# Two heads' scores in one two-bank PSUM tile, their six matmuls tied in order

## The chip, the cores and the metric

The kernel runs on one core of one Trainium2 chip. What counts is device time in microseconds (us) of one execution, the median of several runs. The core's engines run side by side, each through its own queue in order: PE (TensorE: matmuls and transposes into PSUM; PEld is its weight load), DVE (VectorE), ACT (ScalarE), POOL (GpSimd) and SP (which here issues most transfers). PSUM has 8 banks; one bank holds 512 fp32 numbers in each of 128 partitions.

## The reference

Two decoder layers over 512 positions of width 1024, all fp32. Layer 0 (mLSTM heads and pooling groups) is not touched. Layer 1, cut to what matters:

```python
q = rmsnorm(q.reshape(hd), g_q)                  # 16 heads x 64
k = rmsnorm((ckv @ w_uk).reshape(hd), g_k); v = (ckv @ w_uv).reshape(hd)
...
score = einsum('bqh,bqhs->bqs', wib, relu(einsum('bqhd,bsd->bqhs', qib, ki)))   # 4 index heads x 64
_, idx = lax.top_k(score, 128)                   # per query, causal
logits = einsum('bqhd,bqkhd->bqhk', qb, k[idx]) * 64 ** -0.5 + bias[idx]
out = softmax(logits) @ v[idx]
return x + (out * silu(z)) @ w_out
```

## The kernel before

Each fp32 matrix is split into a high and a low part (`_h`, `_l`), and a product takes three matmuls: high by high, high by low, low by high. The kernel computes all causal keys and masks those that the top-k leaves out.

Layer 1 runs by the list `ORDER` of steps: `i` (index scores of one block of 128 queries), `s` (top-k rounds on DVE), `q`, `k`, `v`, `z` (projections), `a` (attention of four heads for one block) and `y` (splitting the gated result for the output projection). Below that list a scheduler orders each engine's instructions: it lays out what is ready by priorities and its own estimate of time, and takes a tile from its pool when a buffer comes free. So an edit at one place can move instructions at others.

`head_pair` (L663) makes the scores of two heads, e = 0 and e = 1. A head has 64 channels, so head 0 lies on partitions 0 to 63 of `q` and `k` and head 1 on 64 to 127, and each matmul uses 64 rows of the array (the shape is shown as 64*128). Two banks of the pool `qk` (`qk=2`, L610) take the heads, one each; the loop writes the matmuls alternately, but the scheduler is free to put others between. `scores` (L676) calls it twice for each of the blocks 1 to 3 and reads each head with a Relu on ACT (L689). `attend` (L784) calls it twice per step, 32 times in all; each head's bank is read by one DVE instruction (L808: it adds the mask and bias tile `cb`, `sel` or `twin` and takes the extreme), then come the exponential (ACT L810), a reciprocal (DVE L811), a scaling (ACT L812), transposes (PE L820, pool `tr`, two banks), their split (ACT L116, DVE L113), the product with v (PE L829 to L831, pool `po`, one bank), and the gate (DVE L835).

With n the number of keys, 256, 384 or 512, there are 38 pairs. The six matmuls of a pair are called here step A (k high, q high), B (k low, q high) and C (k high, q low), each for two heads.

The last projection (`dense_ch4`, L202, called at L852) accumulates four output tiles in two banks of `mm` and two of `qk`; `store` (L845) reads each (L848).

Of the kernel before, what the change touches and what calls it, by code (L numbers as in the profile page):

```python
# [2 lines left out]

# [5 lines left out]
F32 = mybir.dt.float32  # L9
# [49 lines left out]
def trunk(ctx: ExitStack, tc: tile.TileContext, a: dict, out: bass.AP):  # L59
    nc = tc.nc  # L60
    V, A, G, T = nc.vector, nc.scalar, nc.gpsimd, nc.tensor
# [5 lines left out]
    ps = {}  # L67
    ps_pools = ExitStack()

    def psum_pools(**banks):  # L70
        ps_pools.close()
        ps.clear()
        for n, b in banks.items():
            ps[n] = ps_pools.enter_context(tc.tile_pool(name="ps_" + n, bufs=b, space=PSUM))
# [4 lines left out]
    def bank(n):  # L79
        return ps[n].tile([128, 512], F32, name=n)  # L80

    def mm():
        return bank("mm")
# [51 lines left out]
    def wtile(shape, loads, queue=nc.sync):  # L135
        n = math.prod(shape)
        raw = wp.tile([128, 1024], F32, name="raw", bufs=3)
        wh = wp.tile([128, 1024], F32R, name="wh")
        wl = wp.tile([128, 1024], F32R, name="wl")

        def view(t):
            t = t[:, :n]
            if len(shape) == 2:
                t = t.rearrange("p (x y) -> p x y", x=shape[0])
            return t
        for sl, src in loads:
            queue.dma_start(view(raw)[:, sl[0], sl[1]], src)
        A.copy(wh[:, :n], raw[:, :n])  # L148
        low_engine[0].tensor_tensor(wl[:, :n], raw[:, :n], wh[:, :n].bitcast(F32), op=ALU.subtract)  # L149
        return view(wh), view(wl)  # L150
# [3 lines left out]
    def wrows(w, r0, nk, c0, n):  # L154
        return w[r0:r0 + 128 * nk, c0:c0 + n].rearrange("(k p) c -> p k c", p=128)
# [8 lines left out]
    def dense_tok(act, ks, cols, evac, groups=(range(NT),)):  # L164


        n = sum(x[2] for x in cols)
        step = min(1024 // n, len(ks))
        ws = {}
        for tts in groups:  # L170
            acc = {t: mm() for t in tts}
            for k0 in range(0, len(ks), step):
                kk = ks[k0:k0 + step]
                if k0 not in ws:
                    ws[k0] = wcols(cols, kk)
                wh, wl = ws[k0]
                for t in tts:
                    for j, k in enumerate(kk):
                        ah, al = act(k)
                        ts = slice(128 * t, 128 * t + 128)  # L180
                        first, last = (k0 + j == 0), (k0 + j == len(ks) - 1)
                        T.matmul(acc[t][:, :n], ah[:, ts], wh[:, j], start=first, stop=False)  # L182
                        T.matmul(acc[t][:, :n], ah[:, ts], wl[:, j], start=False, stop=False)  # L183
                        T.matmul(acc[t][:, :n], al[:, ts], wh[:, j], start=False, stop=last)  # L184
                    if k0 + step >= len(ks):
                        evac(t, acc[t])
# [7 lines left out]
    def part_ch(act, w, ks, ps):  # L194
        wh, wl = w
        for j, k in enumerate(ks):
            ah, al = act(k)
            T.matmul(ps, wh[:, j], ah, start=(k == 0), stop=False)  # L198
            T.matmul(ps, wh[:, j], al, start=False, stop=False)  # L199
            T.matmul(ps, wl[:, j], ah, start=False, stop=(k == NK - 1))  # L200

    def dense_ch4(act, w, hf, evac, alloc):  # L202

        acc = [alloc(c) for c in range(4)]
        for k0 in range(0, NK, 2):
            wh, wl = wtile([2, 512], [((ALL, ALL), wrows(w, 128 * k0, 2, 512 * hf, 512))])
            for c in range(4):
                cs = slice(128 * c, 128 * c + 128)
                part_ch(act, (wh[:, :, cs], wl[:, :, cs]), (k0, k0 + 1), acc[c])
                if k0 == NK - 2:  # L210
                    evac(4 * hf + c, acc[c])
# [8 lines left out]
    xn = lambda k: (xn_h[:, k], xn_l[:, k])  # L220
# [105 lines left out]
    w_in, w_out = a["e_w_in"], a["e_w_out"]  # L326
# [280 lines left out]

    w_in, w_out = a["o_w_in"], a["o_w_out"]
    w_uk, w_uv = a["o_w_uk"], a["o_w_uv"]
    psum_pools(mm=2, bg=1, qk=2, tr=2, po=1)  # L610
    GR = ((0, 1), (2, 3))
    p2 = ctx.enter_context(tc.tile_pool(name="p2", bufs=1))
    zy = p2.tile([128, 8, S], F32, name="zy")
# [46 lines left out]
    def ckv_proj():  # L660
        dense_tok(xn, range(NK), [(w_in, 1024, 256)], ev_ckv, GR)

    def head_pair(q, k, n):  # L663

        p = [bank("qk"), bank("qk")]
        for j in range(3):
            for e in range(2):
                es = slice(64 * e, 64 * e + 64)
                T.matmul(p[e][:, :n], q(es, j), k(es, j), start=(j == 0), stop=(j == 2))  # L669
        return p  # L670

    near = {0: tmask}
    far = {}
# [2 lines left out]
    def scores(i):  # L676
        n = 128 * (i + 1)
        qs = slice(128 * i, 128 * i + 128)
        acc = sel[i] = (p2 if i == 3 else p1).tile([128, n], F32, name=f"sel{i}")
        G.memset(acc[:, :n - 128], 0.0)  # L680
        G.tensor_copy(acc[:, n - 128:], tmask)
        pair = {}
        for h in range(4):
            if h % 2 == 0:
                pair = head_pair(lambda e, j: (qi_h, qi_h, qi_l)[j][e, h // 2, qs],
                                 lambda e, j: (ki_h, ki_l, ki_h)[j][e, :n], n)
            p = pair[h % 2]
            rl = t1.tile([128, 512], F32, name="relu", tag="cb")
            A.activation(rl[:, :n], p[:, :n], AF.Relu)  # L689
            V.scalar_tensor_tensor(acc, rl[:, :n], wi[:, i, h:h + 1], acc, op0=ALU.mult, op1=ALU.add)  # L690
# [93 lines left out]
    def attend(c, i):  # L784
# [6 lines left out]
        for pr in range(2):  # L791
            probs = []
            pq = head_pair(lambda e, j: (q_h, q_h, q_l)[j][e, pr, qs], lambda e, j: (k_h, k_l, k_h)[j][e, pr, :nn], nn)
            for e in range(2):
                hd = 2 * pr + e
# [46 lines left out]
    step = dict(i=scores, c=ckv_proj, q=q_proj, k=k_proj, v=v_proj, z=z_proj, s=select, a=attend, y=y_split)  # L842
# [6 lines left out]
        nc.scalar.dma_start(out[128 * c:128 * c + 128], o)  # L849

    for hf in range(2):
        dense_ch4(xn, w_out, hf, store, lambda c: bank(("mm", "qk", "mm", "qk")[c]))  # L852


def layout(inputs):
# [34 lines left out]
```

## Time and profile before

| | before |
|---|---|
| median of 3 runs | 774.74 us (774.5 to 776.12) |
| the profiled execution | 773.58 us, of which the span from first to last instruction 771.8 us |
| PE busy | 751.6 us (97%) |
| DVE, ACT, POOL busy | 464.8 (60%), 398.1 (52%), 304.7 us (39%) |
| chain that ended last | PE 84%, DVE 9% |

Layer 1's attention work stands between 488 and 740 us of the span, the last projection mostly behind it. "Busy" of PE counts a matmul from its start to its modelled end, and matmuls overlap; what one costs is read from the distance between the starts of neighbours.

### The profile page before, as it was taken

Reading aid. Unit: us, or ns where it says so; the run is one execution under the profiler, and the core shown is the slowest. Engines: PE = TensorE matmul, PEld = TensorE weight load, DVE = VectorE, ACT = ScalarE, POOL = GpSimd, SP = SyncE. Lnnn points to the kernel's source line nnn. Section 1 sums busy time; section 2 is a strip of 40 time slices with the busy share of each in tenths; the row PEclk is TensorE's granted clock in tenths of the full one; section 3 lists DMA queues with packets and bytes.
Section 4 is the critical chain, followed back from the end, with each engine's and each line's share of the span. In section 5 each row is a group of like instructions: output and inputs, shape, how many; then the busy total and the mean of one; then the engine's idle time right before and its main releaser. Section 6 shows DMA issues by size and latency. Waiting matters only on the chain.

```text
span 771.8 us, 11177 instructions
## 1 busy us (share of the span) xinstructions
PE 751.6 (97%) x4123; PEld 631.6 (82%) x4123; DVE 464.8 (60%) x988; ACT 398.1 (52%) x778; POOL 304.7 (39%) x246
## 2 busy tenths in 40 slices
PE   7989999999999999999999999998999999999988
PEld 5887888887888889888888888987788888887766
DVE  6686534344727765147224572599999978877531
ACT  6445333282445543355433353545667688887620
POOL 5545448732003020131363393445124555472241
PEclk9999999999999999999999999999999999999999
DMA  7523342345332313332322244422321221020051
GB/s 222 155 75 84 84 108 74 105 122 150 106 86 69 87 63 110 82 96 87 89 84 61 88 154 123 111 69 69 82 69 42 69 69 55 9 91 13 28 192 54
DMA packets 83990, 69.20 MB, mean 90 GB/s; under 512 B 3884, under 2 KB 71900, under 8 KB 83936
## 3 DMA queue, kind: packets, MB, share of 16 engines
q1 hardware_dynamic: 82144, 65.83, 29.6%
q10 hardware_dynamic: 1760, 2.66, 1.0%
q8 instruction: 32, 0.52, 0.3%
q14 instruction: 22, 0.18, 0.1%
q0 software_dynamic: 32, 0.01, 0.0%
HBM read 64.25 MB, written 4.23 MB: 89 GB/s over the span
## 4 chain that ended last, share of the span: by engine, by line
PE 84%; DVE 9%; ACT 2%; DMA 2%; issue 2%; POOL 1%; SPq 1%; DVEq 0%; ACTq 0%; POOLq 0%
PE mm L198 13%; PE mm L199 13%; PE mm L200 12%; PE mm L182 8%; PE mm L183 8%; PE mm L184 8%; PE qk L669 5%; PE tr L820 2%; PE po L829 2%; PE po L831 2%; DVE sel L698 1%; DVE m L697 1%; DMA raw<-in_e_w_in_dram 1%; PE po L830 1%; DVE wl L149 1%
## 5 line engine op out<-in xcount | busy, mean ns | idle before, releaser
L149 POOL TENSOR_TENSOR wl<-raw,wh 128x1024 fp32r<-128x1024 f32 (+4 forms) x65 | 148.7, 2290 | 274.4 <-ACT wh L148 230.6
L148 ACT CAST wh<-raw 128x1024 fp32r<-128x1024 f32 (+4 forms) x117 | 113.4, 971 | 172.8 <-PE mm L199 52.3
L198 PE MATMUL mm<-xn_h,wh 128*128 128x512 f32 x336 | 132.8, 397 | 3.1 <-DVE v_l L363 2.0
L200 PE MATMUL mm<-xn_h,wl 128*128 128x512 f32 x336 | 132.6, 395 | 0.0
L199 PE MATMUL mm<-xn_l,wh 128*128 128x512 f32 x336 | 132.3, 394 | 0.0
L183 PE MATMUL mm<-wl,xn_h 128*128 128x256 f32 (+2 forms) x384 | 123.9, 323 | 0.0
L184 PE MATMUL mm<-wh,xn_l 128*128 128x256 f32 (+2 forms) x384 | 123.2, 322 | 0.0
L182 PE MATMUL mm<-wh,xn_h 128*128 128x256 f32 (+2 forms) x384 | 121.6, 325 | 1.0 <-DVE xT L595 0.9
L149 DVE TENSOR_TENSOR wl<-raw,wh 128x1024 fp32r<-128x1024 f32 (+2 forms) x52 | 66.0, 1269 | 63.2 <-ACT wh L148 62.7
L182 PEld LDWEIGHTS mm<-wh,xn_h 128*128 128x128 f32 x384 | 72.0, 189 | 9.2 <-ACT wh L148 1.3
L183 PEld LDWEIGHTS mm<-wl,xn_h 128*128 128x128 f32 x384 | 72.3, 188 | 7.0 <-issue 1.1
L184 PEld LDWEIGHTS mm<-wh,xn_l 128*128 128x128 f32 x384 | 72.2, 188 | 6.7 <-issue 0.7
L198 PEld LDWEIGHTS mm<-xn_h,wh 128*128 128x128 f32 x336 | 63.2, 189 | 17.1 <-DVE v_l L363 2.1
L199 PEld LDWEIGHTS mm<-xn_l,wh 128*128 128x128 f32 x336 | 63.3, 188 | 14.5 <-issue 0.6
L200 PEld LDWEIGHTS mm<-xn_h,wl 128*128 128x128 f32 x336 | 63.3, 188 | 13.8
L200 PE MATMUL mm<-y_h,wl 128*128 128x512 f32 x128 | 50.1, 393 | 0.6 <-DVE wl L149 0.6
L199 PE MATMUL mm<-y_l,wh 128*128 128x512 f32 x128 | 50.4, 394 | 0.0
L198 PE MATMUL mm<-y_h,wh 128*128 128x512 f32 x128 | 48.9, 395 | 0.9 <-ACT y_h L116 0.9
L504 DVE SCALAR_TENSOR_TENSOR cv<-mm,s_conv,cv 128x511 f32<-128x511 f32 (+2 forms) x48 | 35.9, 747 | 16.3 <-ACT cv L502 15.3
L810 ACT ACTIVATE lg<-lg,st 128x128 f32<-128x128 f32 (+3 forms) x64 | 35.8, 561 | 6.1 <-DVE st L808 5.9
L812 ACT ACTIVATE lg<-lg,st 128x128 f32<-128x128 f32 (+3 forms) x64 | 34.0, 557 | 7.4 <-DVE st L811 7.4
L805 POOL TENSOR_TENSOR cb<-sel,abias 128x256 f32<-128x256 f32 x32 | 24.5, 770 | 30.1 <-DVE st L808 22.1
(272 smaller groups left out, 1578.0 us busy)
## 6 DMA issues: line engine op xcount, KB each, us to landing
raw<-in_e_w_in_dram SPq DMA_DIRECT2D x52, 512.0 KB, 3.8
raw<-in_o_w_in_dram SPq DMA_DIRECT2D x18, 512.0 KB, 3.9
raw<-in_e_w_out_dram SPq DMA_DIRECT2D x16, 512.0 KB, 3.8
raw<-in_o_w_out_dram SPq DMA_DIRECT2D x8, 512.0 KB, 3.6
xT<-in_xT_dram SPq DMA_DIRECT2D x8, 256.0 KB, 4.2
x_one<-xT SPq DMA_DIRECT2D x8, 256.0 KB, 3.0
abias<-lines SPq DMA_DIRECT2D x4, 512.0 KB, 4.2
o_sb<-x_one SPq DMA_DIRECT2D x8, 256.0 KB, 4.4
```

The costliest lines, as they stand in the source:

```text
L148: A.copy(wh[:, :n], raw[:, :n])
L149: low_engine[0].tensor_tensor(wl[:, :n], raw[:, :n], wh[:, :n].bitcast(F32), op=ALU.subtract)
L182: T.matmul(acc[t][:, :n], ah[:, ts], wh[:, j], start=first, stop=False)
L183: T.matmul(acc[t][:, :n], ah[:, ts], wl[:, j], start=False, stop=False)
L184: T.matmul(acc[t][:, :n], al[:, ts], wh[:, j], start=False, stop=last)
L198: T.matmul(ps, wh[:, j], ah, start=(k == 0), stop=False)
L199: T.matmul(ps, wh[:, j], al, start=False, stop=False)
L200: T.matmul(ps, wl[:, j], ah, start=False, stop=(k == NK - 1))
L504: V.scalar_tensor_tensor(u[:, j:], ps[:, :S - j], w[:, 3 - j:4 - j], u[:, j:], op0=ALU.mult, op1=ALU.add)
L669: T.matmul(p[e][:, :n], q(es, j), k(es, j), start=(j == 0), stop=(j == 2))
L810: A.activation(lg[:, :n], lg[:, :n], AF.Exp, scale=-1.0, bias=st[:, 0:1], accum_out=st[:, 1:2])
L812: A.activation(lg[:, :n], lg[:, :n], AF.Copy, scale=st[:, 2:3])
```

## The change

The pool `qk` now holds one tile of two banks in place of two tiles of one bank. `head_pair` takes that one tile, head e in bank e. A new function `together` issues the six matmuls in the order A0 A1 B0 B1 C0 C1: each but the first is created under high priority, and each is tied to the one before it by a dependency without a semaphore (`NoSync`), which fixes the order on the engine and adds no wait. The tile comes free when both heads have been read. In the last projection both `qk` accumulators of one half (output tiles 1 and 3 of four) share such a tile.

```diff
-    psum_pools(mm=2, bg=1, qk=2, tr=2, po=1)
+    psum_pools(mm=2, bg=1, qk=1, tr=2, po=1)
...
+    def together(steps):
+
+        last = steps[0]()
+        for step in steps[1:]:
+            with tc.high_priority():
+                ins = step()
+            tc.add_manual_dep(ins.ins, last.ins.name, mybir.DependencyInfo(
+                mybir.DependencyClass.NoSync, mybir.DependencyReason.DATA), reason="together")
+            last = ins
+
     def head_pair(q, k, n):
 
-        p = [bank("qk"), bank("qk")]
-        for j in range(3):
-            for e in range(2):
-                es = slice(64 * e, 64 * e + 64)
-                T.matmul(p[e][:, :n], q(es, j), k(es, j), start=(j == 0), stop=(j == 2))
-        return p
+        p = ps["qk"].tile([128, 2, 512], F32, name="qk")
+        rows = (slice(0, 64), slice(64, 128))
+        together([partial(T.matmul, p[:, e, :n], q(es, j), k(es, j), start=(j == 0), stop=(j == 2))
+                  for j in range(3) for e, es in enumerate(rows)])
+        return p[:, 0], p[:, 1]
...
     for hf in range(2):
-        dense_ch4(xn, w_out, hf, store, lambda c: bank(("mm", "qk", "mm", "qk")[c]))
+        two = ps["qk"].tile([128, 2, 512], F32, name="qk")
+        dense_ch4(xn, w_out, hf, store, lambda c: two[:, c // 2] if c % 2 else mm())
```

No instruction is added or taken away. On every engine the order up to the first index scores is the same; behind them it differs on PE, DVE, ACT and POOL. In the changed file lines up to L608 move down by one, the score matmuls stand at L666 and L669, and lines from L672 on move down by ten (L808 is L818, L835 is L845).

**Place 1, PE, a pair of 256 keys in the second group of four heads.** Before (`mm` is another projection's accumulator, `qk_5697` and `qk_5698` are the two heads' banks):

```order
L183 MATMUL mm_5971<-wl_6005,xn_h_84 128x256
L669 MATMUL qk_5697<-ak_h_4891,aq_h_4973 128x256
L669 MATMUL qk_5697<-ak_l_4892,aq_h_4973 128x256
L669 MATMUL qk_5697<-ak_h_4891,aq_l_4974 128x256
L182 MATMUL mm_5972<-wh_5974,xn_h_84 128x256
L183 MATMUL mm_5972<-wl_5975,xn_h_84 128x256
L669 MATMUL qk_5698<-ak_h_4891,aq_h_4973 128x256
L669 MATMUL qk_5698<-ak_l_4892,aq_h_4973 128x256
L669 MATMUL qk_5698<-ak_h_4891,aq_l_4974 128x256
L184 MATMUL mm_5972<-wh_5974,xn_l_85 128x256
```

The same pair in the changed kernel:

```order
L185 MATMUL mm_5412<-wh_5371,ckv_l_4075 128x256
L666 MATMUL qk_5684<-ak_h_4885,aq_h_4967 128x256
L669 MATMUL qk_5684<-ak_h_4885,aq_h_4967 128x256
L669 MATMUL qk_5684<-ak_l_4886,aq_h_4967 128x256 x2
L669 MATMUL qk_5684<-ak_h_4885,aq_l_4968 128x256 x2
L183 MATMUL mm_5953<-wh_5956,xn_h_84 128x256
```

Two stretches of three with two projection matmuls between became one stretch of six. Of the 38 pairs, 37 now stand as such a stretch, and one of 512 keys is cut into AABB and CC; before, the 228 score matmuls stood in 65 stretches.

**Place 2, PE, a pair of 256 keys in the third group of heads.** Before (two banks, head after head, nothing between):

```order
L184 MATMUL mm_6722<-wh_6754,xn_l_85 128x256
L669 MATMUL qk_6483<-ak_h_5374,aq_h_5969 128x256
L669 MATMUL qk_6483<-ak_l_5375,aq_h_5969 128x256
L669 MATMUL qk_6483<-ak_h_5374,aq_l_5970 128x256
L669 MATMUL qk_6484<-ak_h_5374,aq_h_5969 128x256
L669 MATMUL qk_6484<-ak_l_5375,aq_h_5969 128x256
L669 MATMUL qk_6484<-ak_h_5374,aq_l_5970 128x256
```

The same pair in the changed kernel:

```order
L183 MATMUL mm_6778<-wh_6726,xn_h_84 128x256
L666 MATMUL qk_6460<-ak_h_5366,aq_h_5951 128x256
L669 MATMUL qk_6460<-ak_h_5366,aq_h_5951 128x256
L669 MATMUL qk_6460<-ak_l_5367,aq_h_5951 128x256 x2
L669 MATMUL qk_6460<-ak_h_5366,aq_l_5952 128x256 x2
L841 MATMUL po_6332<-pt_l_6339,av_h_6113 128x256
```

Head after head became step after step. Five pairs stand before as this one does.

**Place 3, PE and DVE, from the last pair of 256 keys (query block 1) of the last group to the next pair.** PE before, from the pair's head 1 to head 0 of the next (`qk_7227`, in the bank that `qk_7185`, head 0, held):

```order
L669 MATMUL qk_7186<-ak_h_6175,aq_h_6719 128x256
L669 MATMUL qk_7186<-ak_l_6176,aq_h_6719 128x256
L669 MATMUL qk_7186<-ak_h_6175,aq_l_6720 128x256
L831 MATMUL po_7005<-pt_l_7025,av_h_6131 128x256
L820 MATMUL tr_7071<-cst_72,lg_7042 128x128
L820 MATMUL tr_7071<-cst_72,lg_7049 128x128
L820 MATMUL tr_7071<-cst_72,lg_7042 128x128
L820 MATMUL tr_7071<-cst_72,lg_7049 128x128
L829 MATMUL po_7055<-pt_h_7061,av_h_6881 128x256
L830 MATMUL po_7055<-pt_h_7061,av_l_6882 128x256
L669 MATMUL qk_7227<-ak_h_6175,aq_h_6719 128x384
```

PE in the changed kernel:

```order
L669 MATMUL qk_7152<-ak_h_6157,aq_l_6692 128x256 x2
L841 MATMUL po_6975<-pt_l_6995,av_h_6113 128x256
L830 MATMUL tr_7040<-cst_72,lg_7011 128x128
L830 MATMUL tr_7040<-cst_72,lg_7018 128x128
L830 MATMUL tr_7040<-cst_72,lg_7011 128x128
L830 MATMUL tr_7040<-cst_72,lg_7018 128x128
L839 MATMUL po_7024<-pt_h_7030,av_h_6853 128x256
L840 MATMUL po_7024<-pt_h_7030,av_l_6854 128x256
L666 MATMUL qk_7193<-ak_h_6157,aq_h_6691 128x384
L669 MATMUL qk_7193<-ak_h_6157,aq_h_6691 128x384
```

DVE before, and then in the changed kernel, around the reads of that pair (`ISA` is L808's instruction and, on a row without `lg`, the reading of its extreme):

```order
L835 TENSOR_TENSOR zy_3890<-po_7005,zy_3890 64x128 x2
L808 ISA lg_7195,st_7196<-qk_7185,cb_7193 128x256
L808 ISA st_7196 128x1
L113 TENSOR_TENSOR pt_l_7062<-tr_7056,pt_h_7061 128x512
L808 ISA lg_7203,st_7204<-qk_7186,cb_7201 128x256
```

```order
L845 TENSOR_TENSOR zy_3890<-po_6975,zy_3890 64x128 x2
L818 ISA lg_7161,st_7162<-qk_7152,cb_7159 128x256
L818 ISA st_7162 128x1
L818 ISA lg_7169,st_7170<-qk_7152,cb_7167 128x256
L818 ISA st_7170 128x1
```

The work between two pairs on PE is the same; before, the next pair's first head needed one read done (of `qk_7185`, whose scores stand eleven rows above the first one shown), now it needs both reads of the pair just computed.

## Rows read from the trace of the kernel before

**Rows 1.** The page: busy time, share of the span and instructions of each engine.
```profile
PE 751.6 (97%) x4123; PEld 631.6 (82%) x4123; DVE 464.8 (60%) x988; ACT 398.1 (52%) x778; POOL 304.7 (39%) x246
```
**Rows 2.** Busy time by stretch: us, per engine with instructions, PE clock, DMA.
```profile
488.00:546.90 58.90, 56.88 (x363) 49.13 (x361) 51.82 (x138) 29.55 (x67) 25.87 (x18) 0.97 0.26 72
546.90:624.50 77.60, 76.32 (x508) 65.96 (x507) 74.33 (x213) 54.46 (x128) 32.49 (x38) 1.00 0.22 60
624.50:740.20 115.70, 112.41 (x734) 92.25 (x732) 84.00 (x271) 92.00 (x223) 56.06 (x62) 1.00 0.16 54
```
**Rows 3.** What PE waited for, 546.9 to 740.2: us, times, longest.
```profile
PE po L829 <- DVE zy L835: 2.2, 4, 1.3
PE mm L182 <- DVE av_l L113: 1.1, 2, 0.8
PE mm L198 <- ACT xn_h L116: 1.1, 1, 1.1
```
**Rows 4.** The score matmuls of step A by size, durations in ns.
```profile
L669 PE MATMUL qk<-ak_h,aq_h x76: 380/437/502, 488.8 to 723.8; 64*128 64x256 f32 x36, 64*128 64x384 f32 x20, 64*128 64x512 f32 x20
```
**Rows 5.** PE in time: start us, us, what; two heads together, 256 keys.
```profile
488.49 0.28 PE L183 MATMUL mm<-wl,xn_h 128*128 128x256 f32 x1
488.61 0.28 PE L184 MATMUL mm<-wh,xn_l 128*128 128x256 f32 x1
488.81 0.39 PE L669 MATMUL qk<-ak_h,aq_h 64*128 64x256 f32 x2
...
489.36 0.38 PE L182 MATMUL mm<-wh,xn_h 128*128 128x256 f32 x1
```
**Rows 6.** PE in time, two heads apart, 256 keys (place 1).
```profile
609.80 0.38 PE L669 MATMUL qk<-ak_h,aq_h 64*128 64x256 f32 x1
...
610.35 0.39 PE L182 MATMUL mm<-wh,xn_h 128*128 128x256 f32 x1
...
610.77 0.38 PE L669 MATMUL qk<-ak_h,aq_h 64*128 64x256 f32 x1
...
611.32 0.38 PE L184 MATMUL mm<-wh,xn_l 128*128 128x256 f32 x1
```
**Rows 7.** PE in time, one head of 384 keys, then one of 512.
```profile
681.31 0.44 PE L669 MATMUL qk<-ak_h,aq_h 64*128 64x384 f32 x1
...
682.03 0.39 PE L182 MATMUL mm<-wh,ckv_h 128*128 128x256 f32 x1
...
649.64 0.50 PE L669 MATMUL qk<-ak_h,aq_h 64*128 64x512 f32 x1
...
650.53 0.39 PE L184 MATMUL mm<-wh,xn_l 128*128 128x256 f32 x1
```
**Rows 8.** PE in time, the untied pair of place 2.
```profile
660.33 0.39 PE L669 MATMUL qk<-ak_h,aq_h 64*128 64x256 f32 x2
...
660.88 0.55 PE L820 MATMUL tr<-cst,lg 128*128 128x128 f32 x3
```
**Rows 9.** PE, then DVE in time, at place 3.
```profile
707.26 0.39 PE L831 MATMUL po<-pt_l,av_h 128*128 128x256 f32 x1
...
708.42 0.36 PE L829 MATMUL po<-pt_h,av_h 128*128 128x256 f32 x1 [0.34 <-DVE zy L835]
...
707.69 0.59 DVE L835 TENSOR_TENSOR zy<-po,zy 64x128 f32<-64x128 f32 x2 [2.18 <-PE po L831]
708.31 0.42 DVE L808 CUSTOM_DVE_ANT_0 lg<-qk,cb 128x256 f32<-128x256 f32 x1
708.66 0.08 DVE L808 DVE_READ_ACCUMULATOR2_ANT st<- 128x1 f32 x1
```
**Rows 10.** DVE in time, a read that came late, of scores begun at 683.16.
```profile
688.37 0.54 DVE L808 CUSTOM_DVE_ANT_0 lg<-qk,cb 128x384 f32<-128x384 f32 x1
```
**Rows 11.** PE in time around a long wait, then the clock behind it by stretch.
```profile
529.12 0.38 PE L182 MATMUL mm<-wh,ckv_h 128*128 128x256 f32 x1 [2.02 <-DVE av_l L113]
...
530.20:533.40 3.20, 3.20 (x15) 2.99 (x15) 3.17 (x8) 2.33 (x5) 2.32 (x2) 0.50 0.00 0
```

More of the change, by code (lines that the diff above doesn't have):

```diff
@@ L2 @@
 from contextlib import ExitStack
+from functools import partial
 import concourse.bass as bass
```

## The prediction

> **What bounds the kernel now.** I read the page's busy shares first: PE is busy for 97% of the span, no other engine above 60% [rows 1]. That is an average, so next the stretches of the attention stage [rows 2]. From 546.9 to 624.5 us DVE, which runs the top-k rounds there, is busy for 74.33 of 77.60 us, as full as PE; from 624.5 to 740.2 us DVE has 84.0 and ACT 92.0 of 115.7 us. Third, what PE waited for between 546.9 and 740.2: 2.2, 1.1 and 1.1 us, 4.4 us in 193 [rows 3]. So PE's own work sets the end, and a microsecond taken out of it there is worth one as long as DVE and ACT can follow; in the first of the two stretches they hardly can.
>
> Last, the score matmuls, by the distance between starts. Two heads together: six matmuls of 256 keys from 488.81 to 489.36, 0.55 us, where "x2" says that both heads' matmuls of a step started side by side [rows 5]. Apart: head 0 alone from 609.80 to 610.35 and head 1 from 610.77 to 611.32, 0.55 us each [rows 6]. One head costs what two cost.
>
> **The change part by part.** *The tied order.* The trace has 38 pairs: 18 of 256 keys, 10 of 384, 10 of 512 (halves of 36, 20 and 20) [rows 4]. A head or a whole pair takes 0.55, 0.72 (681.31 to 682.03) and 0.89 us (649.64 to 650.53) [rows 5, 7]. Following all score rows in time, 14 pairs already run with their heads side by side. Twenty-four are cut. Fourteen of these are two clean halves: 8 of 256, 4 of 384, 2 of 512, and each saves one half, 8 × 0.55 + 4 × 0.72 + 2 × 0.89 = 9.1 us. The other ten are cut inside a head or overlap in part; they save 0.2 to 1.1 us each, by their rows 5.4 us together, less 0.2 for the pair of 512 that stays cut in the new order. That makes 14.3 us.
>
> *Fewer entries.* The first score matmul starts 0.20 us after the matmul before it, where ordinary neighbours of that size lie 0.12 apart (488.49, 488.61, 488.81) [rows 5], so an entry costs about 0.09; behind transposes, which lie 0.03 to 0.11 apart, it costs more, and I take 0.11. The stretches fall from 65 to 39: 26 × 0.11 = 2.9 us (0.09 gives 2.3, 0.17 gives 4.4). PE's work falls by **17.2 us**, 16.4 to 18.5.
>
> *What was tied already.* Place 2 is a pair queued head after head. Its rows show both heads of step A side by side at 660.33, and the transposes behind the six at 660.88, 0.55 us later [rows 8]: the second head overtook two matmuls of the first. Five pairs stand so, and I count no saving for them. The Trainium skill, "TensorE: Matmul & The Clock Gate", section "Part 3: Packing small matmuls — row/col tiling", says that matmuls keep program order in start and end. By that rule these five would be cut pairs and the sum 3 us larger; the trace disagrees, and the sum goes by the trace.
>
> *Where the gain falls.* By the pairs' places, 0.5 us before 546.9, 4.5 in the first stretch and 12.2 in the second. In the first, DVE's 74.33 us of work stay, so at most 77.60 − 74.33 = 3.3 us can come off [rows 2]; the changed order on DVE puts about 3 us of other work behind the last top-k round, which lets PE run on a little. I take 2.5. In the second, 115.7 − 12.2 = 103.5 us would leave DVE 81% and ACT 89% busy: neither is the bound, both are queues with less room.
>
> *The shared tile.* The next pair on PE now waits until both heads are read, where its head 0 waited for one bank. What is queued behind the waiting matmul is all of PE: projections, transposes, products with v; DVE, ACT and the gate wait for those in turn. How long does a read take to come? Often none at all; the worst seen began at 688.37 for a head of 384 keys whose matmuls began at 683.16 and ended 0.72 later, so after 4.5 us [rows 10]. From the new order, with the distances of the trace, I counted PE's work between the end of each pair and the next: 26 of 37 gaps hold over 2 us, 11 hold 0.8 to 2.0. Place 3 is one of the shortest. By the same place before, DVE's gate starts 0.43 us after the start of the last product (707.26, 707.69), the first read 0.62 later (708.31), and its engine is free for the second 0.35 after that (708.66) [rows 9]. A second read of 0.42, and 0.14 for the release (the gate ends at 708.28, PE resumes at 708.42), leave the tile free 1.96 us after that product's start. PE is held to 1.16 us there by the next product's own wait (708.42), as before, and then issues two products, 0.12 and 0.20: it stands for about 0.5 us. So the bounds are nothing for each of the 11 (reads at once) and some 3.5 us (4.5 and a read of 0.5, less 1.5 us of work in such a gap); the prompt end is nearer, since most reads in the trace follow within 2 us, and I take 0.4 × 11 = **4.4 us** lost.
>
> *The rest costs nothing.* The tie sets no semaphore. DVE's, ACT's and POOL's instructions are the same in number and size; they move. In the last projection the second half's tile needs tile 3 of the first half stored; the new order puts twelve 512-column matmuls of another accumulator in between, about 2.8 us, against a store of 0.7. If that cover were gone it would cost 1 us once. SP's queue changes in one place, among the last loads of the residual.
>
> **Sum.** 0.5 + 2.5 + (12.2 − 4.4) = 10.8 us off the profiled execution's 773.58 us, which lies 1.8 above its span: 762.8. The median of the runs, 774.74, lies 1.2 above that execution, and the same gain from there gives 763.9. I say 763.4.
>
> **The rivals.** *Everything arrives.* PE never waits more than now, and the first stretch yields too: 773.6 − 17.2 = 756.4, to 757.5 from the median. For it: 4.4 us of waits in 193 us even with DVE 96% busy. Against it: DVE and ACT have no more slack than above.
>
> *The readers become the bound.* If DVE and ACT queue up in both stretches, half or more of the gain turns into waits: 0.5 + 1 + 5 = 6.5 us, 767 to 768, at worst 771. For it: ACT at 89% and a chain of six steps per pair across four engines. Against it: the orders put two or three pairs between scores and their transposes. The Trainium skill, "TensorEngine Tiling (Array Packing)", section "Performance Considerations", warns of just this: tiling speeds up TensorE but not the reading of PSUM. In the first stretch the trace bears it out, in the second it leaves room.
>
> *The one tile makes it slower.* Each of the 11 short gaps would have to cost 1.6 us more on PE to eat 17.2 us; at the worst lateness, 3.5 us each, the loss is 38 us less 17.2, slower by 21, near 795. Long waits cost twice: behind the 2.02 us wait that ended at 529.12, PE ran at a granted 0.50, that is 1.2 GHz, from 530.2 to 533.4 [rows 11], and 3.2 us at half rate lose another 1.6. It decides from an average of 1.6 us.
>
> *It doesn't do what it says.* Nothing happens if the pairs are still cut. The order excludes it for 37 of 38, and rows 5 show that adjacent heads run side by side.
>
> **How the numbers follow.** Forecast (759.5 to 766.5) 0.55; everything arrives (756 to 759.5) 0.13; the readers bind (766.5 to 773) 0.21; nothing to tell 0.05; slower 0.06. Faster or slower by 0.2%, 1.5 us, is about what a measurement of this kernel can tell from no change: faster 0.88, same 0.06, slower 0.06. The range 757 to 770.5 leaves out a part of the full gain, the worse half of the readers' case, and the last two: 0.05 + 0.04 + 0.11 = 0.2.
>
> **What would show it.** After: step A rows all "x2", score stretches near 39 and their time from first start to what follows near 26 us in place of 40; about 0.5 us of wait in front of score matmuls at some ten places, released by L818. The first stretch should shrink by 2 to 3 us, the second by 7 to 9. If the waits on L818 are above 8 us in sum, or a clock of 0.50 shows in the second stretch, the readers' rival holds; if below 1 us, the full gain. It would be wrong altogether if the new order on DVE and ACT holds PE up at places that have nothing to do with scores.

## The result, and the profile after

The changed kernel takes 767.2 us (median of four runs, 766.2 to 769.5), the kernel before beside it 775.4: a ratio of 0.990, 95% interval 0.987 to 0.993, 8.2 us less. The forecast was 763.4, with a range of 757.0 to 770.5: the sign and the range held, but some 3 us of the expected gain (11.3 from the median) are missing. The profiled execution took 766.22 us with a span of 764.4, against 773.58 and 771.8 before, so the two traces differ by 7.4.

The page of the changed kernel, busy time by engine, answers to [rows 1]:

```profile
PE 735.8 (96%) x4123; PEld 621.1 (81%) x4123; DVE 469.8 (61%) x988; ACT 396.2 (52%) x778; POOL 304.2 (40%) x246
```

The busy time by stretch of the changed kernel, cut at the same places of the program as [rows 2] (first score pair, first pair of the attention, first pair of 512 keys, resumption of PE for the last projection), and then the last projection of the kernel before, which [rows 2] do not reach. Columns: stretch, its length, busy time of each engine with its instructions, granted clock, DMA share, GB/s:

```profile
487.80:545.70 57.90, 54.39 (x354) 46.77 (x353) 51.98 (x140) 28.81 (x64) 25.35 (x18) 1.00 0.25 71
545.70:624.00 78.30, 72.71 (x510) 63.66 (x509) 75.60 (x213) 54.35 (x130) 32.78 (x38) 1.00 0.21 60
624.00:730.75 106.75, 100.17 (x730) 85.21 (x729) 86.52 (x269) 90.06 (x222) 56.38 (x62) 1.00 0.21 67
730.75:764.40 33.65, 29.81 (x120) 23.82 (x120) 5.96 (x9) 2.10 (x2) 4.80 (x2) 0.95 0.22 79
```

```profile
740.20:771.80 31.60, 27.75 (x120) 22.48 (x120) 5.94 (x9) 2.10 (x2) 4.81 (x2) 1.00 0.33 115
```

Length less the first busy column is PE's idle time. The first stretch did not shrink: 78.30 us after 77.60, with PE idle for 5.59 us in place of 1.28, while DVE is still nearly full (75.60 of 78.30). The second fell from 115.70 to 106.75 us. The last projection, unchanged work, grew by 2.05 us, and its clock column says 0.95.

One pair of 256 keys in the changed kernel (place 1, which [rows 6] show apart), and the wait behind it; then DVE and POOL at the same moment:

```profile
599.80 0.38 PE L666 MATMUL qk<-ak_h,aq_h 64*128 64x256 f32 x1
599.80 0.38 PE L669 MATMUL qk<-ak_h,aq_h 64*128 64x256 f32 x1
600.02 0.28 PE L669 MATMUL qk<-ak_l,aq_h 64*128 64x256 f32 x2
600.14 0.28 PE L669 MATMUL qk<-ak_h,aq_l 64*128 64x256 f32 x2
601.74 0.57 PE L754 MATMUL bg<-cst,q_n 128*128 128x128 f32 x2 [1.31 <-DVE q_n L750]
```

```profile
599.50 2.42 DVE L750 TENSOR_TENSOR q_n<-q_n,q_r 128x256 f32<-128x256 f32 x2
598.94 2.37 POOL L150 TENSOR_TENSOR wl<-raw,wh 128x1024 fp32r<-128x1024 f32 x1 [1.81 <-ACT wh L149]
```

Both heads start together, as the tie intends. The time won is gone at once: PE waits 1.31 us for two products that DVE needs 2.42 us for, where one alone mostly takes 0.42. A subtraction on POOL runs beside them; the section on the prediction comes back to it.

What PE waited for from the first pair of the attention to the end of the second stretch, us, times, longest, the largest eight groups; it answers to [rows 3]:

```profile
PE mm L199 <- ACT xn_h L117: 2.6, 1, 2.6
PE mm L183 <- DVE av_l L114: 2.0, 3, 0.9
PE po L839 <- DVE zy L845: 1.5, 4, 0.8
PE bg L754 <- DVE q_n L750: 1.3, 1, 1.3
PE qk L666 <- DVE st L818: 1.1, 3, 0.5
PE po L841 <- DVE pt_l L114: 0.9, 1, 0.9
PE mm L199 <- ACT q_n L737: 0.8, 1, 0.8
PE mm L183 <- ACT q_n L737: 0.5, 1, 0.5
```

The shared tile's own wait is the row `qk L666 <- DVE st L818`: 1.1 us in three places; before the attention one pair of index scores waited another 0.7 us for the Relu that reads its tile. Of the first stretch's 5.5 us DVE released 3.5 and ACT 2.0 (three reads of `q_n` and one of `lg`), so DVE is not the only engine that PE waits for there. The largest is a single wait at the very end. There, the changed kernel's DVE, POOL and PE in time, and the clock of the 3.4 us behind:

```profile
726.79 0.59 DVE L845 TENSOR_TENSOR zy<-po,zy 64x128 f32<-64x128 f32 x2 [0.32 <-PE po L841]
727.42 2.25 DVE L114 TENSOR_TENSOR xn_l<-zy,xn_h 128x256 fp32r<-128x256 f32 x1
729.68 0.59 DVE L845 TENSOR_TENSOR zy<-po,zy 64x128 f32<-64x128 f32 x2
730.74 0.43 DVE L114 TENSOR_TENSOR xn_l<-zy,xn_h 128x256 fp32r<-128x256 f32 x1 [0.47 <-ACT xn_h L117]
727.04 2.35 POOL L150 TENSOR_TENSOR wl<-raw,wh 128x1024 fp32r<-128x1024 f32 x1 [1.89 <-ACT wh L149]
```

```profile
727.84 0.28 PE L841 MATMUL po<-pt_l,av_h 128*128 128x256 f32 x1
730.76 0.80 PE L199 MATMUL mm<-xn_h,wh 128*128 128x512 f32 x1 [2.64 <-ACT xn_h L117]
...
730.80:734.20 3.40, 3.40 (x8) 2.75 (x9) 0.37 (x1) 0.00 (x0) 0.00 (x0) 0.50 0.02 5
```

One `xn_l` took 2.25 us and its fellow 0.43. The last gate (729.68) stood behind the long one in DVE's queue, the last projection waits for that gate, and after the wait PE ran at half clock, 1.2 GHz, for 3.4 us, which lost another 1.7.

From the first score pair on, the account of the two traces is this. PE's busy time falls from 272.6 us (273.4 by [rows 2] and the last projection, less 0.8 ahead of the first pair) to 257.1, by 15.5. Of that the 228 score matmuls, each from its start to the next start on PE less idle time, account for 40.5 − 27.0 = 13.5. PE's idle time rises by 9.1: 1.5 in the stretch before the attention, 4.3 in the first, 3.3 in the second (3.29 to 6.58). Together 6.4 us less; the other 1.0 us came before the first score pair, in work that the change does not touch. Behind that pair the half clock is in both traces once, 3.4 us long: before at 530 [rows 11], now at 731. Ahead of it the kernel before has one more, at 7.9 us, which may be a part of that 1.0 us. More than half of what the tying saved on PE came back as waiting, little of it on the shared tile.

### The profile page after: what moved, and what is told of

It is laid out like the page before. It is cut to its first block, busy times and chain, and to the rows that moved or that the text cites. A ratio compares the mean times of both kernels' runs of the same rounds, so it can differ in the third digit from the quotient of the medians.

```text
span 764.4 us, 11158 instructions
## 1 busy us (share of the span) xinstructions
PE 735.8 (96%) x4123; PEld 621.1 (81%) x4123; DVE 469.8 (61%) x988; ACT 396.2 (52%) x778; POOL 304.2 (40%) x246
## 4 chain that ended last, share of the span: by engine, by line
PE 71%; DVE 19%; ACT 4%; issue 3%; DMA 2%; POOL 1%; SPq 0%; DVEq 0%; ACTq 0%; POOLq 0%
PE mm L199 12%; PE mm L201 12%; PE mm L200 12%; PE mm L183 7%; PE mm L184 7%; PE mm L185 7%; DVE sel L708 3%; DVE m L707 2%; DVE wl L150 2%; DVE q_n L750 1%; DVE lg L818 1%; PE tr L830 1%; DVE pt_l L114 1%; DMA mb<-m_line 1%; DVE sel L700 1%
## 5 line engine op out<-in xcount | busy, mean ns | idle before, releaser
L126 POOL TENSOR_TENSOR q_r<-q_ss,mhalf 128x8 f32<-128x8 f32 x16 | 27.4, 1713 | 17.4 <-DVE q_ss L123 17.1
```

Of the source, the lines that this page charges most:

```text
L126: G.tensor_tensor(dst, ss, mhalf[:, :n], op=ALU.pow)
```

## The experiments

The theory after reading the two traces: the tied pairs give what they should; the shared tile costs little; the waits are for DVE, which is the bound in the first stretch; the tail lost a collision between DVE and POOL. The rivals: the shared tile eats the gain, or the changed order alone makes the waits.

**The tie with two tiles of one bank.** The shared tile is undone, the tie stays; the last projection takes its banks as before.

```
-        p = ps["qk"].tile([128, 2, 512], F32, name="qk")
+        p = [bank("qk"), bank("qk")]
...
-        together([partial(T.matmul, p[:, e, :n], q(es, j), k(es, j), ...
+        together([partial(T.matmul, p[e][:, :n], q(es, j), k(es, j), ...
```

> The tied order with two tiles of one bank each, as before the change. The order of the engine shows 53 stretches of score matmuls (39 with the shared tile, 65 before): 23 pairs stand whole, in 13 the first matmul of head 0 goes ahead alone, since its bank comes free earlier, and the other five follow. Theory (the shared tile costs little: what waits for L818 in the trace after is 1.1 us in sum): such a lone first matmul costs about 0.25 us of step and 0.11 for the entry, 13 x 0.36 = 4.7 us, so the version is slower than the changed kernel by 1 to 5 us, 768 to 772. Rival (the shared tile eats part of the gain, the 4.4 us of the prediction's sum or more): without it the version is faster than the changed kernel by 2 to 5 us, 762 to 765.

Measured: 772.4 us, ratio 0.996 (0.995 to 0.998). The theory's direction holds, the size is just past its upper end (5.2 us): most of the gain goes with the shared tile. In the two traces only 3.0 us of the difference lie behind the first score pair (279.6 us from there, 276.6 in the changed kernel, which has 3.4 us at half clock there where this one has none); the rest came ahead of it, in work that neither edit touches. One pair of it, PE in time:

```profile
721.28 0.38 PE L666 MATMUL qk<-ak_h,aq_h 64*128 64x256 f32 x1
...
721.96 0.38 PE L669 MATMUL qk<-ak_h,aq_h 64*128 64x256 f32 x1
721.96 0.50 PE L669 MATMUL qk<-ak_l,aq_h 64*128 64x256 f32 x2
722.18 0.39 PE L669 MATMUL qk<-ak_h,aq_l 64*128 64x256 f32 x2
```

Head 0's first matmul went ahead alone 0.68 us before its partner, since its bank was free and the other was not (DVE began to read that one at 721.40). The score matmuls take 33.3 us here, 27.0 with the shared tile. So the one tile is not mainly the price of the change; it is what makes both heads ready at the same time.

**The shared tile without the tie.**

```
-        together([partial(T.matmul, p[:, e, :n], q(es, j), k(es, j), ...
-                  for j in range(3) for e, es in enumerate(rows)])
+        for j in range(3):
+            for e, es in enumerate(rows):
+                T.matmul(p[:, e, :n], q(es, j), k(es, j), start=(j == 0), stop=(j == 2))
```

> The shared tile of two banks without the tie. The order shows 44 stretches of score matmuls, 32 of the 38 pairs whole: with one tile both heads become ready together. Theory (what counts is how many pairs stand whole): six cut pairs cost about 0.5 us each and five entries 0.11, 3 to 4 us above the changed kernel, 769 to 772, and clearly below the kernel before. Rival (the high priority of the tie brings the gain, by putting scores ahead of other work): no gain over the kernel before, 773 to 776.

Measured: 766.4 us, ratio 0.988 (0.986 to 0.990). Neither expectation: it is at least as fast as the changed kernel. Set beside runs of nearly the same mean granted clock (0.995, 0.992 to 0.993, 0.990) it is 2.4 to 3.3 us below it. From its first score pair on:

```profile
488.20:762.10 273.90, 259.18 (x1713) 221.44 (x1711) 218.21 (x627) 176.11 (x415) 117.97 (x120) 0.98 0.22 68
```

PE is busy for 259.2 us, 2.1 more than with the tie (the score matmuls alone 28.2 in place of 27.0), but idle for 14.7 in place of 19.5. Of the 2.1 us 1.7 are a second stretch of half clock in this trace (3.4 us at 528.5, besides the one at 729.9), so at equal clock the tie saves PE about 0.4 us of work here. It puts the matmuls of a pair ahead of other ready work, and the 4.8 us of idle time are more than that. In the order of the program, the tie's dependences without the high priority change nothing: PE, DVE, ACT and POOL then have the order of this kernel without any tie. So the high priority is what sets the two kernels apart, though no run shows the tie without it.

**Half the top-k rounds, after and before.**

```
-        for _ in range(4):
+        for _ in range(2):
             m8 = t1.tile([128, 8], F32, name="m8")
```

> The changed kernel with two top-k rounds in each part in place of four, so half of the selection is left out: 24 rounds fewer, by the rows of MAX8 and MATCH_REPLACE8 about 29 us less on DVE, some 14 of them in the first stretch. To be set against the next kernel, which is the same in the kernel before. Theory (in the first stretch DVE was the bound, and the tying's 4.5 us there turned into waits for av_l, q_n and pt_l, 7.0 us in place of 1.7): the difference between the two grows from 8.2 to 12 or 13 us, and PE's waits in the first stretch fall below 3 us. Rival (the waits come from the changed order, whatever DVE has to do): the difference stays at 7 to 9 us.

> The kernel before with two top-k rounds in each part in place of four, so half of the selection is left out. Both theories: PE is the bound here, with 1.7 us of waits in the first stretch and 8.4 in all of the attention stage and the end, so 29 us less on DVE bring 1 to 3 us: 772 to 774.

Measured: 764.1 and 769.6 us; the difference is 5.5, not 12. The expectation on the whole fell. The first stretch of each, the changed kernel first:

```profile
546.80:617.30 70.50, 68.31 (x484) 60.28 (x483) 51.18 (x152) 54.18 (x128) 31.36 (x37) 1.00 0.23 64
544.40:617.70 73.30, 71.67 (x465) 60.85 (x464) 51.14 (x154) 52.11 (x124) 29.77 (x37) 1.00 0.25 68
```

In the stretch itself it held: with DVE at 51 us PE's idle time in the changed kernel falls to 2.19 us (5.59 with all rounds), and the changed kernel's stretch is now 2.8 us shorter than the other's, where it was 0.7 longer. The stretches no longer hold the same work, though (484 and 465 matmuls, 510 and 508 with all rounds), so the order has changed along with the load on DVE, and the rival is not excluded by this run. What fell was the other half: the kernel before gained 6 us and not 1 to 3, because its order changed with the edit as well. It has 55 stretches of score matmuls in place of 65, 23 of them with all six in place of 15, and they take 36.7 us in place of 40.5: part of what the change brings came there without it.

**The products q_n on POOL, after and before.** This takes 10.1 us off DVE in the changed kernel's first stretch, 7.4 in the other's, and leaves nothing out.

```
-                V.tensor_tensor(qn[u], qn[u], ru, op=ALU.mult)
+                G.tensor_tensor(qn[u], qn[u], ru, op=ALU.mult)
```

> The changed kernel with the 32 products q_n (128x256, mean 0.62 us, median 0.42 on DVE) on POOL in place of DVE, nothing left out: 14 of them, 8.8 us of DVE, lie in the first stretch, where DVE is busy for 75.6 of 78.3 us. POOL, with 32 of 78 us there, takes about 0.73 for each. To be set against the next kernel, the same in the kernel before; the order keeps 38 stretches of scores here and 63 there. Theory (DVE holds PE up in the first stretch): PE's idle time there falls from 5.6 us to under 3, the whole gains 2 to 4 us, 763 to 765. Rival (the waits are those of the chains through the engines, which POOL's slower product makes longer by 0.3 us): no gain or a loss, 767 to 770.

> The kernel before with the 32 products q_n on POOL in place of DVE. Both theories: PE is the bound, with 1.3 us of idle time in the first stretch, so it gains at most 1.5 us or loses a little: 773.5 to 776. By the theory that DVE eats the gain of the tying in the first stretch the distance to the changed kernel with the same edit grows from 8.2 to 10 or 12 us; by the rival it stays or shrinks.

Measured: 767.9 (0.989 to 0.993) and 774.6 us (0.997 to 1.000). The changed kernel gains nothing, and the distance between the two shrinks from 8.2 to 6.7 us, as the rival has it. Its first stretch and the part from there to its last score pair, then the same of the kernel before with the edit:

```profile
546.60:619.40 72.80, 69.51 (x484) 60.79 (x483) 65.55 (x193) 56.62 (x131) 38.78 (x50) 1.00 0.23 62
619.40:713.50 94.10, 89.32 (x680) 76.68 (x679) 74.61 (x230) 81.17 (x198) 57.60 (x72) 1.00 0.15 49
```

```profile
546.00:620.60 74.60, 73.65 (x480) 63.34 (x479) 66.98 (x191) 54.40 (x127) 37.33 (x50) 1.00 0.22 61
620.60:722.50 101.90, 101.44 (x690) 83.80 (x689) 73.92 (x234) 84.80 (x204) 57.80 (x72) 1.00 0.14 45
```

The second part in the changed kernel without the edit:

```profile
624.00:712.70 88.70, 85.84 (x654) 73.74 (x654) 76.99 (x242) 80.81 (x199) 49.18 (x59) 1.00 0.16 52
```

PE's idle time in the first stretch falls from 5.59 to 3.29 us, but 4.78 us stand behind it, where there were 2.86. Over the two parts together the idle time is 8.1 us against 8.4. Of the 4.78 us 3.0 are the row `qk L666 <- DVE st L818`, six times: in this order the shared tile's own wait is 3.3 us in all, where it was 1.1. Relieving DVE by this much moves the waits; it does not remove them. (Behind the first score pair this trace has 10.2 us at half clock, the changed kernel's 3.4, so the two lengths are not to be compared as they stand.)

**One more copy for the values on ACT, after and before.** The largest group of waits at accumulators was the one for `av_l`. Here the accumulator is free after a copy by ACT.

```
-        dense_tok(ck, range(2), [(w_uv, 256 * c, 256)],
-                  lambda t, ps: split(v_h[:, t], v_l[:, t], ps[:, 0:256]), GR)
+        def ev(t, ps):
+            v = t1.tile([128, 256], F32, name="v_tok", tag="q_n", bufs=4)
+            A.copy(v, ps[:, 0:256])
+            split(v_h[:, t], v_l[:, t], v)
+        dense_tok(ck, range(2), [(w_uv, 256 * c, 256)], ev, GR)
```

> The changed kernel, in which the projected values leave PSUM by one more copy on ACT (128x256, about 0.4 us, 16 of them) and are split into av_h and av_l from that copy, so that the accumulator no longer waits for DVE's subtraction behind the top-k rounds. PE's waits for av_l are the largest group after the change: 3.8 us, six times. Theory (the gain of the tying went into waits for reads that stand in DVE's queue): the group goes, 2 to 4 us are gained, 763.5 to 765.5. Rival (PE then waits at the next place for the same DVE work, since DVE is the bound there): the waits turn up under other names, the time stays at 766 to 768.

> The kernel before with the same extra copy of the projected values. Its waits for av_l are 3.3 us, 2.0 of them the one wait that ended at 529.12, behind which the clock was at 0.50 for 3.4 us. Theory: that wait goes too, 2 to 4 us, 771 to 773.5, so the distance to the changed kernel with the same edit stays at 8. Rival (no DVE bound before the change, so here the edit brings its full worth and there nothing): the distance shrinks to 5 or 6.

Measured: 771.4 and 779.7 us, both 4 us slower. Between its first pair of the attention and its last, the changed kernel with this edit waited for:

```profile
PE qk L666 <- DVE st L821: 2.2, 4, 1.1
PE po L844 <- DVE pt_l L114: 1.7, 3, 0.7
PE po L842 <- DVE zy L848: 1.5, 3, 0.7
PE bg L754 <- DVE q_n L750: 1.2, 1, 1.2
```

The group is gone, but the first two rows are twice what they were (1.1 and 0.9), and the other two have stayed; all four are DVE's. Another 1.2 us are waits for the new copies themselves. The rival of the first expectation holds: the waits turn up under other names. The distance between the two kernels stays at 8.3. What makes both slower by 4 us is not settled: sixteen copies of 0.4 us on ACT, a third user of the four `q_n` buffers, and a new order came together, and the changed kernel's trace has 10.2 us at half clock behind its first score pair, in place of 3.4.

**The collision in the tail.** One low part of the last weights, which is needed only late in the last projection, waits on POOL until the last `xn_l` is written. The orders of PE, DVE and ACT stay the same to the row, here and in the two kernels further down.

```
+        if late:
+            G.tensor_copy(wl[:, 0:1], xn_l[:, 7, 0:1])
         low_engine[0].tensor_tensor(wl[:, :n], raw[:, :n], wh[:, :n].bitcast(F32), op=ALU.subtract)
...
-            wh, wl = wtile([2, 512], [((ALL, ALL), wrows(w, 128 * k0, 2, 512 * hf, 512))])
+            wh, wl = wtile([2, 512], [((ALL, ALL), wrows(w, 128 * k0, 2, 512 * hf, 512))], late=act is xn and hf == 1 and k0 == 2)
```

> The changed kernel, with one low part of the last projection's weights (second half of the columns, second piece; it is used some 15 us later) held back on POOL until the last piece of xn_l is written; PE's, DVE's and ACT's orders are the same to the row. In the changed kernel this POOL subtraction ran from 727.04 to 729.39, and DVE's xn_l of 128x256 beside it took 2.25 us where its fellows take 0.42; the last gate stood behind it, and PE waited 2.64 us and then ran at a granted 0.50 from 730.8 to 734.2. Theory (the two instructions, both with two inputs from SBUF, got in each other's way, and the tail's loss comes from that): xn_l takes 0.42, PE's wait falls by about 1.4 us to 1.2, and without the long wait the clock stays at 1.0, which gives 1.7 more: 2.5 to 3.5 us below the changed kernel, 763.7 to 764.7. Rival 1 (only the wait, the clock falls all the same): 1.4 us, 765.5 to 766. Rival 2 (xn_l was slow for another reason): no difference, 766.5 to 768.

Measured: 765.3 us, ratio 0.987 (0.985 to 0.989), 1.9 below the changed kernel. DVE, PE and POOL at the place, and the clock behind it:

```profile
728.12 0.43 DVE L114 TENSOR_TENSOR xn_l<-zy,xn_h 128x256 fp32r<-128x256 f32 x1
728.86 0.59 DVE L847 TENSOR_TENSOR zy<-po,zy 64x128 f32<-64x128 f32 x2 [0.32 <-PE po L843]
728.23 0.35 PE L841 MATMUL po<-pt_h,av_h 128*128 128x256 f32 x1 [0.78 <-DVE zy L847]
729.94 0.50 PE L201 MATMUL mm<-xn_h,wh 128*128 128x512 f32 x1 [1.12 <-ACT xn_h L117]
730.75 2.37 POOL L152 TENSOR_TENSOR wl<-raw,wh 128x1024 fp32r<-128x1024 f32 x1
730.50:733.90 3.40, 3.40 (x9) 2.65 (x8) 0.58 (x1) 0.00 (x0) 2.54 (x2) 0.50 0.03 8
```

With POOL out of the way `xn_l` takes 0.43 us and PE's wait falls from 2.64 to 1.12. The clock falls all the same, behind waits of 0.78 and 1.12: rival 1, 0.2 us below its 765.5. So the collision is shown, and the half clock came without the long wait too.

**The same in the kernel with both edits, and in the untied one.**

> The changed kernel with both edits: the extra copy of the values on ACT and the one low part of the last weights held back on POOL, which alone gave 1.9 us. Theory (the two lie in different stretches and add): 2 to 4 us and 1.9, 761.5 to 763.5. Rival (the extra copy only moves the waits): 765 to 766, as with the second edit alone.

> The shared tile without the tie, which ran in 766.4 us, with the one low part of the last weights held back on POOL as before. Its tail has the same picture: 2.62 us of wait and 3.4 us at a granted 0.50. Theory (the collision on DVE and POOL is a thing of the tail, whatever the order of the scores): 1.9 us again, 764 to 765. Rival: the tail's order differs here and nothing is gained, 766 to 767.

Measured: 768.5 us with the extra copy, 2.9 below the 771.4 without the tail's edit, above both expectations; and 762.7 us for the shared tile without the tie, ratio 0.984 (0.982 to 0.985), 3.6 below the 766.4 and below the 764 that was expected. The tail's edit gave 1.9, 2.9 and 3.6 us in three different orders. In each of the three pairs of traces PE's last wait falls from 2.6 to 1.1 us, so 1.5 us belong to the collision; the rest goes along with different shares of half clock and is not shown to come from the edit (the two runs of the untied kernel at a mean clock of 0.995 and 0.996 lie 1.4 apart). The wait of 2.6 us stands in every trace with the shared tile and without the tail's edit, five in all, and in none of the five with two banks, where it is 1.1; why POOL's subtraction falls on that moment with the shared tile is not shown. The last kernel beats both kernels of this case by 4.5 and 12.8 us. It keeps the shared tile, which alone gave the whole gain, and PE is idle for 12.8 us from its first score pair on:

```profile
488.50:760.70 272.20, 259.38 (x1712) 221.63 (x1711) 216.16 (x627) 176.08 (x415) 118.26 (x121) 0.99 0.23 68
```

## Why the prediction was right in sign and 3 us short

**PE's work, 17.2 us: nearly right.** The order has the 39 stretches, the stretches' time is 27.0 us (about 26 forecast, from 40), and PE's busy time fell by 15.5 us, a little below the lower bound of 16.4. (The bounds take the 0.2 us of the cut pair off twice; by the terms as stated they are 16.6 and 18.7.) Of the 15.5 us 13.5 lie in the score matmuls, 14.3 forecast; the other 2.0 lie outside them, where the forecast has 2.9 for the entries.

**The first stretch, 2.5 us of 4.5: wrong.** This is the term that failed most. The stretch grew by 0.7 us. The limit read from [rows 2], that DVE's 74.33 us stay, was the right one, but it was used as a floor that the stretch could sink to. DVE's busy time itself came out at 75.60, which left 2.7 us of room, and PE, running ahead, met reads that weren't done. DVE released 3.5 of the 5.5 us of waits there, 1.3 of them through the product that ran beside POOL's subtraction, and ACT the other 2.0. That DVE's load is the reason for most of it is borne out by the runs with half the top-k rounds (5.59 us of idle time become 2.19), but not shown apart from the order, which changed in them too.

**The shared tile, 4.4 us: too dear, and its place was taken.** The waits on L818 are 1.1 us in three places (1.8 with the wait for the Relu), not 0.5 at ten. In other orders of the tied kernel they are 2.1 us (half the top-k rounds), 2.2 (the extra copy) and 3.3 (`q_n` on POOL), so the term was there and its size hangs on what else holds PE up. The second stretch shrank by 8.95 us, within its 7 to 9, but what PE waited for there was mostly something else: the last projection's `xn_h`, the gates, `pt_l`. The forecast put nearly the right sum on the wrong wait, which was luck. The run with two banks shows that the tile is even where the gain comes from: a tie between two banks that come free at different times lets one head start alone. The prediction gave the whole 14.3 us to the tying and only a cost to the tile.

**"The rest costs nothing": wrong by 1.5 us.** The prediction looked at how many instructions DVE and POOL have, which is unchanged, and at what the last projection's tiles wait for, and not at which of them fall on the same moment. In the changed kernel the last `xn_l` falls on a weight part on POOL, 2.25 us instead of 0.42; then PE waits for it in the end, where nothing covers the wait. That is 1.5 us (2.64, where 1.12 stands once the POOL instruction is held back, and stood before); holding the instruction back gave 1.9 us. The half clock behind it, 1.7 us, is not to be added: it came with the shorter wait too, and the kernel before has one of its own at 530.

The Trainium skill, "SBUF — State Buffer", section "Who interferes with whom", says that a DVE instruction with two SBUF inputs contends with a GpSimd instruction that reads SBUF, and that the port pair which the two share is an exclusive lock. The trace agrees: the long `xn_l` ended at 729.67, 0.28 us after POOL's instruction (727.04 and 2.35), and the two `q_n` together at 601.92, 0.61 after POOL's (598.94 and 2.37). In the kernel before, gates with one input from PSUM ran beside POOL's subtractions at their usual length:

```profile
732.82 7.23 POOL L149 TENSOR_TENSOR wl<-raw,wh 128x1024 fp32r<-128x1024 f32 x3 [9.01 <-ACT wh L148]
735.70 0.59 DVE L835 TENSOR_TENSOR zy<-po,zy 64x128 f32<-64x128 f32 x2 [3.79 <-PE po L831]
737.00 0.84 DVE L113 TENSOR_TENSOR xn_l<-zy,xn_h 128x256 fp32r<-128x256 f32 x1
```

The `xn_l` among them took twice its time and ended 0.28 us after the second of the three subtractions (737.56). Such collisions were there before the change: a `q_n` at 596.44 took 2.34 us beside a subtraction on POOL, and PE did not wait for it.

**The rivals.** The time lies in the band given to the readers' rival (766.5 to 773, a chance of 0.21), just above the forecast's own (759.5 to 766.5, 0.55). By its mechanism it is that rival in the first stretch, where all of the gain became waits, and not in the second, where 8.95 of 12.2 us stayed. Its sign, above 8 us on L818, did not come: the waits stand at other reads, and a sign tied to one line missed them. The last sign of the prediction, by which it would be wrong altogether, came in good part: of the 12.2 us that PE is idle between 545.7 and 730.75 only 1.3 stand in front of scores. So the sign of the result follows from the mechanism forecast (PE's work fell by nearly what was said), while the size lies in the range by a sum whose waits are in other places. "Everything arrives" is excluded by 9.1 us of new idle time, "slower" by the 1.1 us on the tile.

What stays open: why the tie's high priority costs more waiting than it saves work, and how much of the waits in both stretches is due to the order alone. Each edit but the one in the tail also changed the order of many other instructions; in the kernel before with half the top-k rounds the new order took 3.8 us off the score matmuls, of a gain of 6.

## What to carry to other kernels

To make two instructions of a pair run side by side, first let them become ready together, by one buffer with one release; here an order on top of that, made by priority, brought no more. Where a second engine is busy for 95% of a stretch, don't count on a gain from the first in that stretch, and look for waits at every read, not only at the one that the change touches. Before calling untouched engines free, look at what falls on the same moment in the last few microseconds, where a single long instruction in front of the last gate is paid in full.

## What was not expected of the hardware

The half clock came and went at the same place of the program. Behind a wait of 2.02 us [rows 11], of 2.64 us (changed kernel), and of 0.78 and 1.12 us (with the tail's edit) PE ran at a granted 0.50, that is 1.2 GHz, for 3.4 us each, which costs up to 1.7. In the kernel before with `q_n` on POOL the same wait of 2.02 us stands at the same place (529.05), and the clock stayed at 1.00. So the prediction's "long waits cost twice" holds in some runs and not in others. At the start of the last projection it is the other way round: in the kernel before, behind waits of 1.30 and 1.12 us, the clock stayed up; in the kernel before with `q_n` on POOL, behind 1.31 and 1.12 us, it fell. The stretches of these two, the clock in the third column from the end:

```profile
740.20:743.60 3.40, 3.40 (x15) 2.82 (x16) 1.09 (x2) 0.00 (x0) 0.00 (x0) 1.00 0.79 296
739.70:743.00 3.30, 3.30 (x9) 2.54 (x8) 0.69 (x1) 0.00 (x0) 0.00 (x0) 0.50 0.53 200
```

In the same time PE starts 15 matmuls in the one and 9 in the other. Of the five kernels with two banks, all with these two waits, it fell in three. A difference of 1.7 us between two single traces can come from this alone. It is in the medians too: of 45 runs of the kernel before, the two at a mean granted clock of 0.998 took 772.8 and 773.1 us, the sixteen at 0.990 took 776.0 on average.
